# SyncE in program order, the finished inverse loaded by GpSimd, and all cross products in a step's first half, in a bidirectional RWKV-7 layer

## The chip, the core and the metric

The kernel runs on one core of one Trainium2 chip. The metric is the device time of one execution in microseconds (us). Five engines work side by side, each with an instruction stream of its own: TensorE (PE, its weight loads are PEld), VectorE (DVE), ScalarE (ACT), GpSimd (POOL) and SyncE (SP), which here does nothing but ask for transfers between the chip's memory (DRAM) and the core.

## The reference

One layer over 128 context and 2048 latent tokens, model width 1024: a normalised and modulated input goes through one projection; half of its channels feed a bidirectional RWKV-7 scan (8 heads of 64, a state of 64 by 64 per head and direction), half a short gated convolution; both are gated, concatenated and projected back onto the residual, and a final normalisation follows.

```python
def step(S, inp):                      # in _wkv, per token, both directions
    r_t, w_t, k_t, v_t, kk_t, a_t = inp
    s_kk = jnp.einsum('bdhij,bdhj->bdhi', S, kk_t)
    S = (S * w_t[..., None, :] - s_kk[..., :, None] * (kk_t * a_t)[..., None, :]
         + v_t[..., :, None] * k_t[..., None, :])
    return S, jnp.einsum('bdhij,bdhj->bdhi', S, r_t)
...
u = jnp.concatenate([ya, yb], axis=-1) @ lp['w_out']     # in _layer
return x + gate * u, s_final
```

## The kernel before

The kernel has two phases. phase1 projects all tokens and leaves in DRAM what the second needs: the scaled keys and queries of each chunk ("ops"), the values ("vt"), gates and a bonus term ("sg", "q") and the finished convolution half ("mixT"). phase2 (line 657 on), which the change is about, scans.

The scan is done in chunks of 64 tokens. A step s of the main loop covers a tile of 128 tokens in the forward direction and one in the backward, 17 steps in all; its two halves step(s, 0) and step(s, 1) are a chunk each, in both directions, for all heads. A half multiplies the state with the chunk's keys (psw, copied into ws), begins the output (psy) and the new state (pst), applies the chunk's inverse (psu, out of zb and ws, copied into sv), and then ends pst (DVE scales it into the next sv) and psy. So a half needs the state of the half before it, and zb.

zb is the inverse of a triangular matrix in each chunk, for 16 pairs of head and direction in a half; it does not depend on the state, so it is prepared two steps ahead, in this chain:

1. cross(u, i, d) for u = s + 2, four of them (C(0) to C(3) in the loop): products of the chunk's keys and queries (psB, psX). ACT copies one part into lab; for the second of each pair (i = 1), SyncE stores the diagonal 32 by 32 blocks into DRAM as "at" (line 728); DVE masks the rest into x and abr.
2. inverse(u): SyncE loads all blocks of the step as ab (line 749, two transfers), GpSimd eliminates in 15 rounds (lines 754 to 769) and stores the inverted blocks zt by four transfers of its own queue (line 774) into "zt" in DRAM.
3. merge(s + 1), a step later: SyncE loads zb (line 829), DVE transposes its blocks into a tile of the tag ws (STREAM_TRANSPOSE), TensorE fills in the block below the diagonal (psU, copied by ACT into the ws tile, then psW, copied into zb).

turn transposes keys (psT, copied into kbt; R(0) to R(3)), load_units loads kb and x for step s + 3 (L(0), L(1); lines 699 and 701), load_v loads sv (line 863).

Into these the loop mixes independent work. piece() records a quarter of a projection job: a job multiplies one tile of 128 tokens (mr, split into the halves mh by ACT and ml by DVE) with the output weights (wo..h and wo..l) in two sums of 12 matmuls, psoc (convolution half, steps 0 to 8) or psoa (scan half, from step 9 on); DVE scales each sum (o) and adds it to the residual tile z. z has two buffers and is loaded from the input x (psoc) or from "z0", where the first half of the projection left it (psoa). Eight pieces, so two jobs, go into a step. In step 9 no job is at hand and the four weight tiles are replaced (weights(), loads at line 1003 into z buffers). F() records a stage of finish(), which normalises a finished tile of the scan (psv, psr, the y operations); its result is the input of a psoa job.

What orders the work: Queue (line 640) wraps an engine. While held is set, each instruction recorded through it gets a dependency on the one recorded before, so TensorE, VectorE and ScalarE run in the program's order; their instructions all show line 648, where Queue calls the engine. SyncE and GpSimd are not held: a scheduler places their instructions by its own simulation. Each engine takes its instructions one at a time, so what waits at the head of SyncE holds up all transfers behind it. A store and a load that touch the same place in DRAM are ordered by waits on the transfer's landing.

Of the kernel before, what the change touches and what calls it, by code (L numbers as in the profile page):

```python
# [632 lines left out]
NST = 17  # L633
# [23 lines left out]
def phase2(K):  # L657
    nc, tc, A, S = K.nc, K.tc, K.A, K.S
    G = nc.gpsimd
    V, P, T = Queue(tc, nc.vector), Queue(tc, nc.scalar), Queue(tc, nc.tensor)  # L660
    D = nc.sync.dma_start
# [82 lines left out]
    def inverse(s):  # L744

        at = S["at"][s]
        ab = tl(O.r, [128, 32, 32], "ab", 2)
        for h in range(2):
            D(ab[h * 64:h * 64 + 64].rearrange("p j i -> p (j i)"), at.rearrange("b u h j i -> (b u h) (j i)"))
# [21 lines left out]
        for c in range(2):  # L771
            for b in range(2):
                x = dst[:, b * 32 + c:b * 32 + 32:2, b * 32:b * 32 + 32]
                G.dma_start(x, zt[c * 64 + b * 32:c * 64 + b * 32 + 32])

    def first(s):
        for d in range(2):
            load_units(s, d)
        for k in UNITS:
            cross(s, *k)  # L780
            yield
            turn(s, *k)
            yield
        inverse(s)
# [40 lines left out]
    def merge(s):  # L825

        zb = tl(O.r, [128, 16, 64], "zb", 2)
        zbs[s] = zb
        D(zb[:], S["zt"][s % 3].rearrange("u h r c -> (h r) u c"))
# [21 lines left out]
    svs = {}  # L851
    ys = {}
# [12 lines left out]
    def step(s, i):  # L865
# [7 lines left out]
        if not last:  # L873
            load_v(*n)
        if n == (1, 0):
            sv = svs[n]
            for h in range(2):
                for d in range(2):
                    D(sv[HR[h], h, d], A["st0"][:, d, h::2, :])
                x = sv[HR[h], h].rearrange("r d p v -> r (d p) v")  # L880
                mn = tl(O.l, [128, 8], "mn", 2)
                V.tensor_reduce(mn[HR[h]], x, mybir.AxisListType.X, ALU.add)
                V.tensor_scalar(mn[HR[h]], mn[HR[h]], -1.0 / 64, None, ALU.mult)
                V.tensor_tensor(x, x, mn[HR[h]].unsqueeze(2).broadcast_to((64, 8, 64)), ALU.add)
# [21 lines left out]
        for h in range(2):  # L906
            P.copy(sv[HR[h], h], u[HR[h]])
        yield
        if not last:
# [32 lines left out]
        if i == 1:  # L942
            zbs.pop(s)
            for d in range(2):
# [6 lines left out]
                elif s < 8:  # L951
                    D(S["ysp"][t], ys.pop(t)[:])
# [64 lines left out]
    def project(j):  # L1017
# [23 lines left out]
        if att:  # L1041
# [8 lines left out]
            D(S["y"][t0:t0 + 128, :], z[:])  # L1050
        else:
            D(S["z0"][t0:t0 + 128, :], z[:])
        yield

    def main():
        setup_rest()
        for e in (T, V, P):
# [8 lines left out]
        def take():  # L1066
# [11 lines left out]
            z = tl(O.w, [128, 1024], "z", 2)  # L1078
            D(z[:], src[t * 128:t * 128 + 128, :])
            j = Ctx()  # L1080
            j.t, j.att, j.x, j.z, j.k, j.headed = t, att, x, z, 0, False
            j.run = project(j)
            nxt.append(j)

        def piece(n=1):
            for _ in range(n):
                if B.load:
# [3 lines left out]
                if not nxt:  # L1091
                    take()
                if not now:
                    if nxt:
                        j = nxt.pop()
                        split(j)
                        now.append(j)
                    continue
                j = now[0]
                if j.k == 2 and nxt:  # L1100
# [4 lines left out]
                if j.k == 4:  # L1105
                    run(j.run)
                    now.clear()
                    if nxt:
                        m = nxt.pop()
                        split(m, m.headed)  # L1110
                        now.append(m)
# [17 lines left out]
        def F(n=1):  # L1129

            if fin:
# [11 lines left out]
        for s in range(NST):  # L1143
# [41 lines left out]
            C(2)  # L1185
            piece()
            R(2)
            L(0)
# [15 lines left out]
            piece(2)  # L1204
            m = merge(s + 1) if s + 1 < NST else iter(())
            next(m, 0), next(m, 0)
# [8 lines left out]
        while now or nxt or waiting:  # L1215
            piece()
        for p in (O.pu, O.q, O.w, O.l, O.pt, O.pg, O.r):
# [54 lines left out]
```

## Time and profile before

| what | value |
|---|---|
| median of 3 runs | 1976.24 us (1975.0 to 1979.27) |
| profiled execution, its own time | 1986.27 us |
| its span, first to last instruction | 1984.5 us |
| mean granted TensorE clock | 0.899 |
| PE, PEld, DVE busy | 1646.4, 1439.3, 1052.3 us |
| ACT, POOL busy | 641.0, 585.6 us |
| main loop | from about 1062 us on |
| steps 2 to 8 (1162 to 1493 us) | 331 us |

In the profile a row of a window names the stretch and then busy time and count by engine. A row of the waits has the engine, what it was about to do, after the arrow what ended the wait, and total us, times and the longest. A row of the timeline is start and duration in us, engine, line, operation, out<-in, shape and count; in brackets stands the idle time just before and what ended it. SPq and POOLq are transfers asked for by SyncE and GpSimd; their duration is the asking, not the transfer.

### The profile page before, as it was taken

The numbers are of one execution on the slowest core, as the hardware profiler recorded it, in microseconds if no ns is written. First come the engines' busy times: TensorE is split into PE (matmuls) and PEld (weight loads), VectorE is DVE, ScalarE is ACT, GpSimd is POOL, SyncE is SP. The second block draws the span as 40 slices with busy tenths as digits, with TensorE's granted clock in tenths as the row PEclk, the third lists the DMA queues.
The fourth block names the chain that finished last, engine by engine and source line by source line (L and its number), as shares of the span: only waits on it lengthen the run. The fifth ranks groups of instructions, "written<-read, shape, count | busy, mean of one in ns | idle before, by whom it ended". The sixth has DMA issues, their size and how long they took to land. (4 is left out here: it accounts for less than half of the span.)

```text
span 1984.5 us, 40833 instructions
## 1 busy us (share of the span) xinstructions
PE 1646.4 (83%) x16646; PEld 1439.3 (73%) x16646; DVE 1052.3 (53%) x1883; ACT 641.0 (32%) x1284; POOL 585.6 (30%) x1096
## 2 busy tenths in 40 slices
PE   5999999999999999988985966788774657877785
PEld 3998899998899998887984754566563435665564
DVE  6988876457673637764433533344332335454454
ACT  4565543244441315541102222222222312323232
POOL 0122200012120002220450544556555553345500
PEclk8999999999999999998996887888887768888787
DMA  8899986658995536789744456566564454553322
GB/s 334 235 231 245 225 241 244 234 125 182 177 198 150 195 144 153 184 188 247 222 144 138 108 150 163 145 183 179 158 177 95 113 143 136 145 142 94 114 85 85
DMA packets 390124, 339.90 MB, mean 171 GB/s; under 512 B 284136, under 2 KB 335208, under 8 KB 375856
## 3 DMA queue, kind: packets, MB, share of 16 engines
q1 hardware_dynamic: 387760, 332.82, 61.7%
q0 software_dynamic: 2176, 4.46, 1.3%
q8 instruction: 131, 2.15, 0.5%
q14 instruction: 57, 0.47, 0.1%
HBM read 215.68 MB, written 121.52 MB: 170 GB/s over the span
## 5 line engine op out<-in xcount | busy, mean ns | idle before, releaser
L769 POOL TENSOR_TENSOR zt<-zt,ztmp 128x30 f32<-128x30 f32 (+7 forms) x510 | 210.4, 412 | 40.0
L648 PE MATMUL psU<-ws,lab 32*32 32x32 f32 x1088 | 37.3, 237 | 172.9 <-DVE ws L648 172.9
L648 DVE TENSOR_TENSOR x<-psX,mx 64x512 f32<-64x512 f32 x136 | 93.6, 688 | 150.6 <-PE psB L648 127.7
L648 PEld LDWEIGHTS psU<-ws,lab 32*32 32x32 f32 x1088 | 33.2, 150 | 181.3 <-issue 172.9
L766 POOL TENSOR_TENSOR ztmp<-ab,zt 128x60 f32<-128x60 f32 (+7 forms) x255 | 137.9, 541 | 20.0
L315 POOL TENSOR_TENSOR shk<-rawl 128x384 f32<-128x384 f32 (+1 forms) x24 | 27.1, 1131 | 319.4 <-ACT rawl L311 311.1
L758 POOL COPY dgp<-ab 128x16 f32<-128x16 f32 x17 | 4.2, 245 | 382.4 <-DMA ab<-scr_at 382.3
L648 PE MATMUL psoa<-woh,ml 128*128 128x512 f32 x136 | 67.2, 494 | 49.4 <-DVE ml L648 49.4
L648 PE MATMUL psoa<-woh,mh 128*128 128x512 f32 x136 | 69.8, 513 | 20.9 <-ACT mh L648 20.9
L648 PE MATMUL psX<-x,kb 64*64 64x128 f32 x1088 | 84.2, 285 | 0.0
L648 PEld LDWEIGHTS psB<-x,kb 64*64 64x64 f32 x1088 | 62.7, 137 | 23.1 <-issue 17.5
L648 PEld LDWEIGHTS psoa<-woh,ml 128*128 128x128 f32 x136 | 32.3, 237 | 64.1 <-DVE ml L648 56.8
L648 PE MATMUL psB<-x,kb 64*64 64x128 f32 x1088 | 74.7, 277 | 3.0 <-DVE abr L648 1.7
L648 DVE TENSOR_TENSOR o<-psoa,gl 128x512 f32<-128x512 f32 x32 | 22.1, 689 | 103.1 <-PE psoa L648 101.7
L648 DVE TENSOR_TENSOR o<-psoc,gl 128x512 f32<-128x512 f32 x32 | 22.0, 687 | 97.5 <-PE psoc L648 97.5
L648 ACT ACTIVATE o<-z 128x512 f32<-128x512 f32 x34 | 21.4, 630 | 156.7 <-issue 90.5
L159 PE MATMUL mmg<-h,w 128*128 128x384 f32 (+1 forms) x192 | 63.4, 330 | 6.5 <-ACT rawc L318 3.9
L159 PE MATMUL mmv<-h,w 128*128 128x384 f32 (+1 forms) x192 | 66.6, 347 | 2.7 <-ACT q1r L313 1.5
L159 PE MATMUL mmk<-h,w 128*128 128x384 f32 (+1 forms) x184 | 61.6, 335 | 8.2 <-DMA w<-scr_wsp 8.2
L648 PE MATMUL psoc<-woh,mh 128*128 128x512 f32 x136 | 65.1, 479 | 0.0
L159 PE MATMUL mmgb<-h,w 128*128 128x384 f32 (+1 forms) x192 | 63.7, 332 | 1.5 <-DMA w<-scr_wsp 1.5
L160 PE MATMUL mmv<-h,w 128*128 128x384 f32 (+1 forms) x192 | 64.8, 337 | 0.0
(298 smaller groups left out, 5366.8 us busy)
## 6 DMA issues: line engine op xcount, KB each, us to landing
w<-scr_wsp SPq DMA_DIRECT2D x68, 1024.0 KB, 7.3
scr_wsp<-w SPq DMA_DIRECT2D x34, 1024.0 KB, 6.3
wr<-in_win SPq DMA_DIRECT2D x34, 512.0 KB, 6.9
kb<-scr_ops SPq DMA_DIRECT2D x34, 512.0 KB, 5.0
x<-scr_ops SPq DMA_DIRECT2D x68, 256.0 KB, 6.6
scr_ops<-sp SPq DMA_DIRECT2D x80, 192.0 KB, 4.6
scr_ops<-sp SPq DMA_DIRECT2D x160, 96.0 KB, 5.1
ab<-scr_at SPq DMA_DIRECT2D x34, 256.0 KB, 4.0
```

Of the source, the lines that this page charges most:

```text
L159: T.matmul(ps[:, :n], w[:, 0, k], hh[:, 0, k, :n], start=k == 0, stop=False)
L160: T.matmul(ps[:, :n], w[:, 0, k], hh[:, 1, k, :n], start=False, stop=False)
L315: G.tensor_tensor(s[:, lo:n].rearrange("p (r c) -> p r c", c=64), rp[:, :R, 0:64], rp[:, :R, 2:66], ALU.add)
L648: r = f(*args, **kw)
L758: G.tensor_copy(dg[:], ab[:].rearrange("p j i -> p (j i)")[:, 1:1024:66])
L766: G.tensor_tensor(tv, ab[:, j:j + 2, j + 2:32].unsqueeze(1).broadcast_to((128, kn, 2, n)), zt[:, :kn, j:j + 2].unsqueeze(3).broadcast_to(( ...
L769: G.tensor_tensor(zt[:, :kn, j + 2:32], zt[:, :kn, j + 2:32], tv[:, :, r], ALU.add)
```

## The change

- SyncE becomes a Queue too and is held from main() on: its transfers are asked for in the order in which the program records them.
- The program's order is rewritten for that: load_v stands behind the u to sv copies of a half, the residual z of a job is loaded by base() at the k = 1 of the job before it (or in ready()), fetch(u), the ab load, is split off inverse(u) and recorded after the psu of the second half and a piece, stores of z0, y and ysp are collected in late and recorded by flush() at the next piece; L(0) and L(1) move back a little; the mean that is subtracted from the first state is computed after the first psu.
- inverse(u) ends with the load of zb on GpSimd's own queue, behind the four stores of zt; merge only picks the tile up.
- C(3) and R(3) go ahead of step(s, 1).
- merge's transposes are recorded ahead of two pieces instead of behind them, one more F() follows psU, head() of the next job comes at k = 3 instead of 2, and ready() lets F() begin a job.

```diff
@@ phase2
-    V, P, T = Queue(tc, nc.vector), Queue(tc, nc.scalar), Queue(tc, nc.tensor)
-    D = nc.sync.dma_start
+    V, P, T, SP = Queue(tc, nc.vector), Queue(tc, nc.scalar), Queue(tc, nc.tensor), Queue(tc, nc.sync)
+    D = SP.dma_start
...
-    def inverse(s):
-
-        at = S["at"][s]
+    def fetch(s):
         ab = tl(O.r, [128, 32, 32], "ab", 2)
         for h in range(2):
-            D(ab[h * 64:h * 64 + 64].rearrange("p j i -> p (j i)"), at.rearrange("b u h j i -> (b u h) (j i)"))
+            D(ab[h * 64:h * 64 + 64].rearrange("p j i -> p (j i)"), S["at"][s].rearrange("b u h j i -> (b u h) (j i)"))
+        return ab
+
+    def inverse(s, ab):
+
         zt = tl(O.r, [128, 16, 32], "zt", 1)
...
                 G.dma_start(x, zt[c * 64 + b * 32:c * 64 + b * 32 + 32])
+        zb = tl(O.r, [128, 16, 64], "zb", 2)
+        zbs[s] = zb
+        G.dma_start(zb[:], S["zt"][s % 3].rearrange("u h r c -> (h r) u c"))
...
     def merge(s):
 
-        zb = tl(O.r, [128, 16, 64], "zb", 2)
-        zbs[s] = zb
-        D(zb[:], S["zt"][s % 3].rearrange("u h r c -> (h r) u c"))
+        zb = zbs[s]
...
+    late = []
+
+    def flush():
+        while late:
+            late.pop(0)()
@@ step
-        if not last:
-            load_v(*n)
-        if n == (1, 0):
...
         for h in range(2):
             P.copy(sv[HR[h], h], u[HR[h]])
+        if not last:
+            load_v(*n)
...
-                    D(S["ysp"][t], ys.pop(t)[:])
+                    late.append(lambda t=t, y=ys.pop(t): D(S["ysp"][t], y[:]))
@@ project
-            D(S["y"][t0:t0 + 128, :], z[:])
-        else:
-            D(S["z0"][t0:t0 + 128, :], z[:])
+        late.append(lambda: D(S["y" if att else "z0"][t0:t0 + 128, :], z[:]))
@@ main
-        for e in (T, V, P):
+        for e in (T, V, P, SP):
             e.held = True
...
+        def base(j):
+
+            j.z = tl(O.w, [128, 1024], "z", 2)
+            D(j.z[:], j.src[j.t * 128:j.t * 128 + 128, :])
+
+        def ready():
+            if not nxt:
+                take()
+            if not now and nxt:
+                j = nxt.pop()
+                if j.z is None:
+                    base(j)
+                split(j, j.headed)
+                now.append(j)
+
         def piece(n=1):
             for _ in range(n):
+                flush()
...
-                if j.k == 2 and nxt:
+                if j.k == 1 and nxt:
+                    base(nxt[0])
+                if j.k == 3 and nxt:
                     nxt[0].headed = True
                     head(nxt[0])
...
         def F(n=1):
 
+            if not B.load:
+                ready()
@@ main, the loop over s
             C(2)
+            R(2)
             piece()
-            R(2)
-            L(0)
+            C(3)
+            R(3)
             F()
             a = step(s, 1)
             next(a), next(a)
-            C(3)
-            if u:
-                inverse(u)
-            R(3)
-            L(1)
+            L(0)
             F()
             next(a)
             piece()
+            if u:
+                ab = fetch(u)
+                inverse(u, ab)
+            L(1)
             F()
             piece()
             next(a), next(a)
             F()
+            m = merge(s + 1) if s + 1 < NST else iter(())
+            next(m, 0)
             piece(2)
-            m = merge(s + 1) if s + 1 < NST else iter(())
-            next(m, 0), next(m, 0)
+            next(m, 0)
+            F()
             piece(2)
             next(m, 0)
             piece()
```

The order on SyncE in step 4, which prepares u = 6. The names have running numbers; at is the store of blocks, lab its source. Before, from just behind the first at store on:

```order
L699 DMA kb_1423_12777<-scr_ops0_57 128x2x512
L1052 DMA scr_z0_68<-z_1396_12387 128x1024
L701 DMA x2_1424_12778<-scr_ops0_57 64x2x512 x2
L701 DMA x3_1434_12921<-scr_ops1_59 64x2x512 x2
L1071 DMA mr_1435_12944<-scr_mixT_64 128x4x128
L1079 DMA z_1436_12946<-in_x 128x1024
L829 DMA zb_1442_13024<-scr_zt_66 128x16x64
L728 DMA scr_at_65<-lab_1414_12680 32x8x32 x4
L699 DMA kb_1433_12920<-scr_ops1_59 128x2x512
L863 DMA sv_1449_13129<-scr_vt_61 64x2x256
L952 DMA scr_ysp_67<-y_1417_12727 128x512
L749 DMA ab_1428_12851<-scr_at_65 64x1024 x2
```

And now, from that first at store on:

```order
L648 DMA scr_at_65<-lab_1414_12642 32x8x32 x4
L648 DMA scr_z0_68<-z_1392_12330 128x1024
L648 DMA scr_at_65<-lab_1418_12695 32x8x32 x4
L648 DMA kb_1429_12862<-scr_ops0_57 128x2x512
L648 DMA x2_1430_12863<-scr_ops0_57 64x2x512 x2
L648 DMA sv_1431_12886<-scr_vt_61 64x2x256 x2
L648 DMA z_1432_12889<-in_x 128x1024
L648 DMA ab_1434_12900<-scr_at_65 64x1024 x2
L648 DMA kb_1439_12964<-scr_ops1_59 128x2x512
L648 DMA x3_1440_12965<-scr_ops1_59 64x2x512 x2
L648 DMA scr_ysp_67<-y_1421_12742 128x512
```

The two at stores have moved together, with a z0 store between them, and ab follows behind one kb, one x, sv and one z load; zb is gone from SyncE, where the second at store and ab stood behind it.

The order on VectorE at the end of step 4, around the transposes of the next step's zb (STREAM_TRANSPOSE, made for psU of step 5). Before:

```order
L648 TENSOR_TENSOR o_1438_12962<-psoc80_12949,gl_10178 128x512
L648 TENSOR_TENSOR z_1405_12507<-z_1405_12507,o_1438_12962 128x512
L648 TENSOR_TENSOR sv_1425_12782<-pst41_12821,pc_10168 64x512 x2
L648 TENSOR_TENSOR o_1440_13018<-psoc81_13005,gl_10178 128x512
L648 TENSOR_TENSOR z_1405_12507<-z_1405_12507,o_1440_13018 128x512
L648 TENSOR_TENSOR ml_1441_13022<-mr_1435_12944,mh_1439_13003 128x512
L648 STREAM_TRANSPOSE ws_1443_13026<-zb_1442_13024 32x512 x2
L648 TENSOR_TENSOR o_1447_13082<-psoc90_13069,gl_10178 128x512
L648 TENSOR_TENSOR z_1436_12946<-z_1436_12946,o_1447_13082 128x512
```

And now:

```order
L648 TENSOR_TENSOR o_1433_12897<-psoc80_12782,gl_10182 128x512
L648 TENSOR_TENSOR z_1407_12517<-z_1407_12517,o_1433_12897 128x512
L648 TENSOR_TENSOR sv_1431_12886<-pst41_12859,pc_10172 64x512 x2
L648 STREAM_TRANSPOSE ws_1441_13012<-zb_1398_12403 32x512 x2
L648 TENSOR_TENSOR o_1443_13025<-psoc81_12969,gl_10182 128x512
L648 TENSOR_TENSOR z_1407_12517<-z_1407_12517,o_1443_13025 128x512
L648 TENSOR_TENSOR ml_1444_13028<-mr_1413_12622,mh_1442_13017 128x512
L648 TENSOR_TENSOR o_1448_13084<-psoc90_13034,gl_10182 128x512
L648 TENSOR_TENSOR z_1432_12889<-z_1432_12889,o_1448_13084 128x512
```

The transposes have moved ahead of the end of the job of tile 8 (psoc81) and of the split of the next job's input (ml); before, they stood behind both. The same sv operation stands ahead of them.

The order on VectorE in step 12, from the masks of the last cross products to the next job's input; the z operation with fg is the final scaling of a psoa job. Before:

```order
L648 SCALAR_TENSOR_TENSOR y_1690_16467<-y_1690_16467,gwh_10162,psr11_17313 128x128 x4
L648 TENSOR_TENSOR y_1690_16467<-y_1690_16467,sg_1742_17134 128x512
L648 TENSOR_TENSOR y_1690_16467<-y_1690_16467,mr_1743_17135 128x512
L648 TENSOR_TENSOR x5_1721_16848<-psX1411_17373,mx_8877 64x4x2x64 x2
L648 TENSOR_TENSOR abr11_1762_17395<-psB1411_17372,mx_8877 128x256
L648 RECIPROCAL rs_1770_17478<-rs_1770_17478 128x8
L648 TENSOR_TENSOR o_1772_17508<-psoa71_17294,gl_10178 128x512
L648 TENSOR_TENSOR z_1729_16957<-z_1729_16957,o_1772_17508 128x512
L648 TENSOR_TENSOR ss_1736_17035<-ss_1736_17035 128x1
L648 RECIPROCAL ss_1736_17035<-ss_1736_17035 128x1
L648 SCALAR_TENSOR_TENSOR z_1729_16957<-z_1729_16957,ss_1736_17035,fg_1676_16268 128x1024
L648 TENSOR_TENSOR ml_1774_17519<-y_1690_16467,mh_1773_17517 128x512
```

And now:

```order
L648 TENSOR_TENSOR o_1756_17316<-psoa71_17090,gl_10182 128x512
L648 TENSOR_TENSOR z_1735_16997<-z_1735_16997,o_1756_17316 128x512
L648 TENSOR_TENSOR ss_1737_17037<-ss_1737_17037 128x1
L648 RECIPROCAL ss_1737_17037<-ss_1737_17037 128x1
L648 SCALAR_TENSOR_TENSOR z_1735_16997<-z_1735_16997,ss_1737_17037,fg_1660_16076 128x1024
L648 TENSOR_TENSOR x5_1729_16908<-psX1411_17325,mx_8877 64x4x2x64 x2
L648 TENSOR_TENSOR abr11_1757_17347<-psB1411_17324,mx_8877 128x256
L648 SCALAR_TENSOR_TENSOR y_1691_16476<-y_1691_16476,gwh_10166,psr11_17358 128x128 x4
L648 TENSOR_TENSOR y_1691_16476<-y_1691_16476,sg_1742_17140 128x512
L648 TENSOR_TENSOR y_1691_16476<-y_1691_16476,mr_1743_17141 128x512
L648 TENSOR_TENSOR ml_1767_17423<-y_1691_16476,mh_1766_17421 128x512
```

The end of the job of tile 7 (psoa71, z with fg) has moved ahead of the x5 mask and of the y operations of finish; ml of the next job stands at the end as before.

More of the change, by code (lines that the diff above doesn't have):

```diff
@@ L783, in first @@
             yield
-        inverse(s)
+        inverse(s, fetch(s))
     def early():
@@ L1108, in piece @@
                     if nxt:
[L1109 to L1111 removed]
+                        ready()
         def head(j):
```

33 lines of the change are left out of this document (15 added, 18 removed).

## The prediction

> **What bounds the kernel now.** First the page: one execution, its span 1984.5 us.
>
> ```profile
> span 1984.5 us, 40833 instructions
> ```
>
> Then the windows, cut where a step of the main loop begins (steps 0–1, 2–8, 9, 10, 11–14, 15 with the tail). The columns are the stretch, its us, busy PE, PEld, DVE, ACT, POOL with counts, the granted clock, the DMA share and GB/s.
>
> ```profile
> 1070.00:1162.00 92.00, 76.50 (x1318) 60.88 (x1319) 41.53 (x70) 25.86 (x50) 26.75 (x56) 0.84 0.48 122
> 1162.00:1493.00 331.00, 247.09 (x4514) 198.91 (x4508) 123.85 (x193) 84.36 (x167) 184.30 (x394) 0.86 0.60 162
> 1493.00:1562.00 69.00, 29.79 (x612) 23.92 (x612) 18.18 (x27) 14.33 (x23) 42.11 (x84) 0.66 0.41 104
> 1562.00:1633.00 71.00, 43.95 (x674) 33.96 (x672) 29.37 (x52) 16.86 (x37) 40.02 (x81) 0.78 0.49 123
> 1633.00:1865.00 232.00, 179.01 (x2689) 140.15 (x2688) 113.63 (x208) 67.40 (x144) 111.08 (x222) 0.82 0.47 127
> 1865.00:1984.50 119.50, 85.39 (x977) 67.46 (x976) 57.77 (x113) 33.56 (x75) 1.85 (x3) 0.84 0.28 89
> ```
>
> No engine is full: in steps 2–8, 331/7 = 47.3 us each, TensorE is idle 84 us, and POOL, which computes the inverses, idles 147. The waits of that stretch (us in total, times, longest) name the partners:
>
> ```profile
> POOL dgp L758 <- DMA ab<-scr_at: 115.6, 8, 24.9
> PE psU L648 <- DVE ws L648: 75.4, 14, 18.8
> SPq L829 <- DMA scr_zt<-zt: 62.0, 7, 17.0
> ```
>
> 75.4 of TensorE's 84 idle us lie before one place, psU, which waits for DVE's transposes of zb, the finished inverse. And POOL waits for its next input, ab, while SyncE stands on the zb load. One turn of the timeline shows that these close a loop:
>
> ```profile
> 1347.27 2.98 SPq L728 DMA_DIRECT2D scr_at<-lab  x4
> ...
> 1392.11 0.38 SPq L829 DMA_DIRECT2D zb<-scr_zt  x1
> 1392.71 2.56 SPq L749 DMA_DIRECT2D ab<-scr_at  x2
> ```
>
> ```profile
> 1358.90 0.20 POOL L758 COPY dgp<-ab 128x16 f32<-128x16 f32 x1 [11.20 <-DMA ab<-scr_at]
> ...
> 1385.95 2.65 POOL L774 DMA_DIRECT2D scr_zt<-zt  x4 [0.30 <-POOL zt L769]
> 1392.09 0.53 POOL L754 MEMSET zt<- 128x512 f32 x1 [3.49 <-DMA scr_zt<-zt]
> 1400.09 0.20 POOL L758 COPY dgp<-ab 128x16 f32<-128x16 f32 x1 [7.13 <-DMA ab<-scr_at]
> ```
>
> The ab of the next inverse is asked for only at 1392.71, right behind the zb of this one. So a turn is ab's trip, POOL's 27.05 us (1358.90 to 1385.95), the stores' landing, and then the same again: 1400.09 − 1358.90 = 41 us here, in which POOL works for 27. POOL is a partner in the loop, not a full engine.
>
> **The step without the loop.** The same turn on TensorE:
>
> ```profile
> 1362.23 1.15 PE L648 MATMUL psw<-sv,x 128*64 128x64 f32 x32
> ...
> 1372.73 0.50 PE L648 MATMUL psoc<-woh,mh 128*128 128x512 f32 x1
> ...
> 1374.22 0.60 PE L648 MATMUL psT<-idt,kb 128*128 128x128 f32 x4
> ...
> 1398.73 0.28 PE L648 MATMUL psU<-ws,lab 32*32 32x32 f32 x2 [10.26 <-DVE ws L648]
> ...
> 1401.21 0.80 PE L648 MATMUL psoc<-woh,mh 128*128 128x512 f32 x1
> ...
> 1406.63 1.21 PE L648 MATMUL psW<-zb,ws 32*32 32x32 f32 x64
> ...
> 1409.36 1.15 PE L648 MATMUL psw<-sv,x 128*64 128x64 f32 x32
> ```
>
> The step is 47.13 us (1362.23 to 1409.36), 10.26 of it the wait. Behind the wait twelve psoc matmuls take 5.42 us (0.45 each); six undisturbed ones took 1.49 (0.25). So the cold clock costs 12 × 0.20 = 2.4, and the warm work is 47.13 − 10.26 − 2.4 = 34.4 us.
>
> What the wait has hidden comes out. DVE has this chain between the last matmul of one projection job and the first of the next:
>
> ```profile
> 1384.72 1.38 DVE L648 TENSOR_TENSOR sv<-pst,pc 64x512 f32<-64x512 f32 x2
> 1388.51 0.69 DVE L648 TENSOR_TENSOR o<-psoc,gl 128x512 f32<-128x512 f32 x1 [2.41 <-PE psoc L648]
> 1389.24 0.69 DVE L648 TENSOR_TENSOR z<-z,o 128x512 f32<-128x512 f32 x1
> 1389.85 0.68 DVE L648 TENSOR_TENSOR ml<-mr,mh 128x512 fp32r<-128x512 f32 x1
> ```
>
> 0.69 + 0.69 + 0.68 = 2.06, now bare once a step, since matmuls of the next job stand ahead of psU and want ml; and I keep 2.0 of the 2.4 for a half clock that such a gap may still cause. T0 = 34.4 + 2.06 + 2.0 = 38.5 us a step.
>
> **The change, part by part.** SyncE in program order with the ab load behind both at stores, the cross products in the first half, and zb on GpSimd together set a new trip, counted from a step's first psw. C(3) ends where the order puts it: C(2) ended 10.5 in (1372.73), then psT 0.6, a piece 1.5, C(3) about 1.1, the lab copy 0.6: the stores are issued at 14.3. Store issue to POOL's start 11.63 (1347.27 to 1358.90, a turn where nothing stood between); POOL 27.05; its stores until POOL goes on 6.14 (1385.95 to 1392.09); the issue of zb on GpSimd and its landing:
>
> ```profile
> L774 POOL DMA_DIRECT2D scr_zt<-zt x68: 648/648/812, 989.2 to 1866.2; - x68
> ```
>
> ```profile
> zb<-scr_zt SPq DMA_DIRECT2D x17, 512.0 KB, 4.7
> ```
>
> No GpSimd load of zb is in the trace; I take one store's 0.65 us and SyncE's landing of 4.7. The bounds: its issue could be as much as all four stores, 2.65, and its other terms 1.7 shorter where the stores land sooner. Sum 14.3 + 11.63 + 27.05 + 6.14 + 0.65 + 4.7 = 64.5 (62.8 to 66.5). The transposes stand 23.9 into the next step (behind the sv pair, done at 1386.10 in a step begun at 1362.23). A wait W lengthens both the step in which the trip runs and that in which it ends: 2W = 64.5 − 38.5 − 23.9 = 2.1, W = 1.0, T = 39.5 (37 to 42, the lower end with no half clock and no wait, the upper with 66.5 and a second bare gap). POOL itself needs 27.05 + 6.14 + 0.65 = 34 a turn, and 39 if it stands for zb's landing too: near T, not above. Steps 2–8 gain 7 × (47.3 − 39.5) = 55; steps 0–1, without the full loop, 92 − 81 = 11; the weights' loads that merge(0) waits for, 3.
>
> The Trainium skill, SBUF — State Buffer, section "A bandwidth-pool intuition that's wrong (but worth ruling out)", speaks against zb on GpSimd: a DMA of GpSimd of some 620 ns alone takes some 3100 beside a copy on VectorE, as its descriptors must wait. The 68 stores above, made while DVE ran tensor_tensors, are 648 to 812 ns, so the trace does not show it; by the rule the sum would be (3.1 − 0.65)/2 = 1.2 more a step, an estimate from that page, 9 us in all.
>
> Steps 9 and 10 have their own rows, first waits, then SyncE's issues:
>
> ```profile
> PE psU L648 <- DVE ws L648: 39.2, 4, 35.7
> ...
> PE psoa L648 <- DVE ml L648: 19.3, 2, 14.8
> ```
>
> ```profile
> 1524.32 0.37 SPq L829 DMA_DIRECT2D zb<-scr_zt  x1
> ...
> 1540.69 1.01 SPq L1003 DMA_DIRECT2D z<-in_wout  x2
> ...
> 1596.78 0.54 SPq L1044 DMA_DIRECT2D fg<-in_fg  x1
> ```
>
> In step 9 the transposes stand on DVE behind the halves of the new weights, whose last two loads were issued only at 1540.69, behind zb, at, kb, x and ab. With zb off SyncE they go when their buffers are free, and the 35.7 us go; what is late next is POOL's trip or the weights' own chain of loads and copies, so I take 47 rather than 40: 69 − 47 = 22. In step 10 the final scaling waited for fg, issued behind ab; in program order it stands between the step's two at stores, ahead of x, sv and ab (the first of the order's places has the same at stores), about 10 us sooner than 1596.78, an estimate by SyncE's place in a step: 14.8 goes nearly whole, with its cold clock: 71 − 54 = 17.
>
> Steps 11–14 wait elsewhere:
>
> ```profile
> PE psoa L648 <- DVE ml L648: 23.2, 8, 5.0
> PE psoa L648 <- ACT mh L648: 13.2, 4, 3.3
> ```
>
> 36.4 us in four steps of 58 at a clock of 0.82. At one of the two job boundaries of a step the job's end on DVE now stands ahead of the last cross products, and TensorE has those to do meanwhile; the other stays, and z now comes by a later load. I take half of the two rows and of the cold clock behind them, 7 a step: 58 to 51 (bounds 46 and 57), 4 × 7 = 28. Step 15 and the tail, where no inverse is left: 2.5. Deferred stores, the state-mean and the extra F() I take at nothing: SyncE stands on a z store's landing ahead of a z load already now, and the at stores come later; without that cover it is one landing, about zb's 4.7, on the trip, 2.4 a step.
>
> Sum: 3 + 11 + 55 + 22 + 17 + 28 + 2.5 = 138.5. The profiled execution took 1986.27; less 138.5 it is 1847.8. The median of the runs, 1976.24, is 0.995 of it: 1838 us.
>
> **The rivals.** (a) The loop stays the bound on POOL's side: GpSimd's zb load holds POOL until landing and the next ab comes in its shadow, T = 43. For it: POOL's 34–39. Against: the ab of the next step is asked for 50 us ahead. Steps 2–8 then gain 30 instead of 55, step 9 about 16: 1838 + 25 + 6 = 1869. (b) The attention steps gain nothing: VectorE's chain and the z load asked at k = 1 stay last at both boundaries: 1838 + 28 = 1866. (c) No half clock is left and the late steps reach 46: 7 × 2.5 + 4 × 5 = 37 less, 1801. The Trainium skill, TensorE: Matmul & The Clock Gate, section "HAM oscillation — how this bites in real kernels", would let the clock drop only behind gaps above some 3.4 us, which favours (c); the trace has not decided it for gaps of 2 us. (d) Slower: SyncE in program order is a single file. The z0 store, which waits for DVE, stands ahead of at stores, and mr ahead of sv; if such a data wait delays at and ab by D, the trip grows by D and a step by D/2. It decides against the change when D passes 2 × 7.8 = 16 us in steps 2–8; at 25 us they lose 7 × 4.7 = 33, steps 9–14 gain half of 67 at most, and with sv or kb late too, nothing: 2009. For it: SyncE stood 62 us on a data wait before. Against: in the new order the z0 store between the at stores belongs to a job whose last DVE operations stand ahead of the step's first cross product. (e) TensorE's wait is not for zb's loop but returns elsewhere, as ml and mh waits, and nothing shows: 1976.
>
> **How the numbers follow.** Forecast 0.58, (a) 0.12, (b) 0.12, (c) 0.08, (d) 0.06, (e) 0.04. The forecast's own bounds (T 37 to 42, late steps 46 to 57) give 1806 to 1868. Low 1800 takes in (c); high 1880 takes in (a) and (b); (d) and (e) are out. A measurement of this kernel tells 0.2%, 4 us, from no change: faster 0.90, same 0.04, slower 0.06.
>
> **What would show it.** Right: psU's wait in steps 2–8 falls from 75.4 to under 20 us, POOL's wait for ab to under 60, the zb load's issue on GpSimd is under 1 us, steps are 39.5 us, and no 35.7 or 14.8 us wait is left in steps 9 and 10. A zb issue near 3 us, or steps of 43 with POOL always busy, is (a); ml and mh waits above 30 us in steps 11–14 is (b). The prediction is wrong if SyncE's longest waits are for DVE's z while POOL stands on ab, or if psU still waits 8 us a step.

## The result, and the profile after

The changed kernel takes 1920.65 us in the median of 4 runs (1913.59 to 1922.74), the kernel before 1977.76 in runs on the same chips (1975.0 to 1987.64): ratio 0.9696, 95% interval 0.9654 to 0.9739. It is faster by 57 us; the forecast was faster by 138, to 1838, with a range of 1800 to 1880. The direction came, and 41% of the size.

The profiled execution took 1919.48 us, its span is 1917.7. The windows of after, cut at the same steps as those of before (0 to 1, 2 to 8, 9, 10, 11 to 14, 15 with the tail):

```profile
1065.00:1159.00 94.00, 79.34 (x1318) 62.35 (x1320) 42.10 (x71) 26.36 (x51) 35.63 (x74) 0.84 0.63 153
1159.00:1471.00 312.00, 236.20 (x4512) 187.60 (x4506) 124.61 (x193) 82.82 (x167) 197.12 (x405) 0.87 0.61 161
1471.00:1525.00 54.00, 31.82 (x618) 25.35 (x618) 19.97 (x29) 15.20 (x26) 32.19 (x66) 0.76 0.59 147
1525.00:1580.00 55.00, 40.98 (x676) 32.44 (x678) 28.22 (x52) 16.92 (x37) 25.71 (x53) 0.84 0.60 154
1580.00:1794.00 214.00, 162.78 (x2688) 128.18 (x2688) 114.82 (x208) 67.46 (x144) 118.41 (x235) 0.84 0.54 139
1794.00:1917.70 123.70, 87.31 (x970) 68.31 (x970) 57.03 (x111) 32.97 (x74) 12.62 (x24) 0.82 0.30 92
```

Set against the rows of before, with what the forecast gave each term:

| stretch | before, us | after, us | gain | forecast |
|---|---|---|---|---|
| up to step 0 | 1070 | 1065 | 5 | 3 |
| steps 0 and 1 | 92 | 94 | −2 | 11 |
| steps 2 to 8 | 331 | 312 | 19 | 55 |
| step 9 | 69 | 54 | 15 | 22 |
| step 10 | 71 | 55 | 16 | 17 |
| steps 11 to 14 | 232 | 214 | 18 | 28 |
| step 15 and tail | 119.5 | 123.7 | −4 | 2.5 |
| sum | 1984.5 | 1917.7 | 67 | 138.5 |

The two spans differ by 67 us, the medians by 57: the profiled execution of before was 10 us above its median. Of the 72 us that are missing in the profile 36 lie in steps 2 to 8. There six of the seven steps now come in pairs, 52 to 54 us and then 35 to 36; the last takes 47.7, the mean is 44.6. One step of 36 us and the one of 53 behind it from the timeline, first SyncE in the step that begins at 1210.7:

```profile
1224.76 2.61 SPq L648 DMA_DIRECT2D scr_at<-lab  x4
1227.47 0.40 SPq L648 DMA_DIRECT2D kb<-scr_ops  x1
1228.03 1.23 SPq L648 DMA_DIRECT2D x<-scr_ops  x2
1229.64 1.71 SPq L648 DMA_DIRECT2D sv<-scr_vt  x2
1231.39 0.59 SPq L648 DMA_DIRECT2D z<-in_x  x1
1232.10 1.11 SPq L648 DMA_DIRECT2D ab<-scr_at  x2
```

The inverse of that ab on GpSimd, begun near the end of this step, and then, in the next one (begun at 1246.8), the transposes it releases on VectorE and what TensorE waits for:

```profile
1242.64 0.66 POOL L760 COPY dgp<-ab 128x16 f32<-128x16 f32 x1 [18.96 <-DMA ab<-scr_at]
...
1270.05 2.62 POOL L776 DMA_DIRECT2D scr_zt<-zt  x4 [0.30 <-POOL zt L771]
1279.20 1.16 POOL L779 DMA_DIRECT2D zb<-scr_zt  x1 [6.54 <-DMA scr_zt<-zt]
...
1281.30 0.20 POOL L760 COPY dgp<-ab 128x16 f32<-128x16 f32 x1
```

```profile
1285.07 1.42 DVE L648 STREAM_TRANSPOSE ws<-zb 32x512 f32<-32x512 f32 x2 [14.13 <-DMA zb<-scr_zt]
1286.51 0.69 DVE L648 TENSOR_TENSOR o<-psoc,gl 128x512 f32<-128x512 f32 x1
1287.24 0.82 DVE L648 TENSOR_TENSOR z<-z,o 128x512 f32<-128x512 f32 x1
1287.98 0.83 DVE L648 TENSOR_TENSOR ml<-mr,mh 128x512 fp32r<-128x512 f32 x1
```

```profile
1288.87 0.79 PE L648 MATMUL psoc<-woh,ml 128*128 128x512 f32 x1 [16.23 <-DVE ml L648]
```

Over steps 2 to 8 the waits are these:

```profile
PE psoc L648 <- DVE ml L648: 54.4, 6, 17.2
PE psU L648 <- DVE ws L648: 14.2, 2, 13.8
POOL dgp L760 <- DMA ab<-scr_at: 49.6, 3, 19.0
```

What the reader is to see: most of the wait has changed its name, from psU for the transposes (75.4 us before) to psoc for ml, because the transposes now stand ahead of the job's end on VectorE and hold it. Its cause is the same zb, and with 68.6 us in both rows it has hardly shrunk. What steps 2 to 8 gained is 8 us of TensorE's idle time (84 to 76 in the windows) and 11 us of its busy time (247 to 236). And the trip of the inverse, from the step's first psw to the transposes, is 1285.07 − 1210.7 = 74.4 us where the prediction had 64.5. GpSimd went on to the next inverse 2.1 us after it asked for zb; its wait for ab, 18.96 here, is one of the long kind of before. The median landings of the loads in the whole run, KB and us, before first:

```profile
kb<-scr_ops SPq DMA_DIRECT2D x34, 512.0 KB, 5.0
x<-scr_ops SPq DMA_DIRECT2D x68, 256.0 KB, 6.6
...
ab<-scr_at SPq DMA_DIRECT2D x34, 256.0 KB, 4.0
```

and after:

```profile
kb<-scr_ops SPq DMA_DIRECT2D x34, 512.0 KB, 8.2
x<-scr_ops SPq DMA_DIRECT2D x68, 256.0 KB, 8.6
...
ab<-scr_at SPq DMA_DIRECT2D x34, 256.0 KB, 8.2
zb<-scr_zt POOLq DMA_DIRECT2D x17, 512.0 KB, 6.1
```

Program order asks for kb, x, sv, z and ab, 2.25 MB, within 6 us, and kb, x and ab land later than before. That gives theory A: the change is limited by its own burst of loads, which makes the trip 10 us longer. Its rivals: B, GpSimd's part of the trip is what is long (the landing of its stores, the asking for zb); C, SyncE in single file costs by its waits or by the place that a transfer has in it.

### The profile page after: what moved, and what is told of

The parts are those of the page before. It is cut to its first block, busy times and chain, and to the rows that moved or that the text cites. A ratio compares the mean times of both kernels' runs of the same rounds, so it can differ in the third digit from the quotient of the medians.

```text
span 1917.7 us, 40711 instructions
## 1 busy us (share of the span) xinstructions
PE 1622.0 (85%) x16646; PEld 1416.9 (74%) x16646; DVE 1057.2 (55%) x1883; ACT 640.4 (33%) x1284; POOL 604.5 (32%) x1113
## 5 line engine op out<-in xcount | busy, mean ns | idle before, releaser
L648 PE MATMUL psoc<-woh,ml 128*128 128x512 f32 x136 | 59.2, 435 | 67.8 <-DVE ml L648 67.0
L648 PE MATMUL psU<-ws,lab 32*32 32x32 f32 x1088 | 32.1, 226 | 84.4 <-DVE ws L648 84.4
L648 PEld LDWEIGHTS psU<-ws,lab 32*32 32x32 f32 x1088 | 29.0, 141 | 92.7 <-issue 88.2
L648 PEld LDWEIGHTS psoc<-woh,ml 128*128 128x128 f32 x136 | 28.5, 209 | 78.1 <-DVE ml L648 70.5
L648 PE MATMUL psoa<-woh,ml 128*128 128x512 f32 x136 | 64.2, 472 | 22.5 <-DVE ml L648 22.5
L648 DVE TENSOR_TENSOR z<-z,o 128x512 f32<-128x512 f32 x68 | 51.6, 758 | 32.3 <-DMA z<-scr_z 23.1
L159 PE MATMUL mmv<-h,w 128*128 128x384 f32 (+1 forms) x192 | 65.7, 342 | 1.1 <-ACT q1r L313 0.6
```

The lines of the kernel that those rows point to most:

```text
L159: T.matmul(ps[:, :n], w[:, 0, k], hh[:, 0, k, :n], start=k == 0, stop=False)
L648: r = f(*args, **kw)
```

## The experiments

Each kernel is the changed one with the edit shown; "..." stands for lines left out. Times are medians beside the kernel before on the same chip, whose medians were 1982.5 to 1984.4 us in these sessions; so compare the ratios.

**Ab asked for first** (e1) and **kb and x last** (e2):

```diff
             C(3)
             R(3)
+            ab = fetch(u) if u else None
...
             if u:
-                ab = fetch(u)
                 inverse(u, ab)
```

```diff
             next(a), next(a)
-            L(0)
...
                 inverse(u, ab)
+            L(0)
             L(1)
```

> The changed kernel with one move: the ab load is recorded right behind the last cross product's turn, ahead of kb, x, sv and z. Theory A (the trip of an inverse is 74 us instead of 64.5 because ab is asked for last in a burst of loads, and lands in 8 to 10 us instead of 4 to 6): ab is asked for about 3 us sooner and lands in under 6, the trip is about 66, steps 2 to 8 fall from 44.6 to about 40 us, the whole by 25 to 35 us to 1887 to 1896. Theory B (the trip is long because of GpSimd's own part: the landing of its stores, then the issue of zb): at most the 3 us of the earlier asking come off the trip, half of that off a step, 1908 to 1920.

> The changed kernel with the first kb and x loads moved behind the ab load, to the second ones; sv and z stay ahead of ab. Theory A (a burst of loads delays what stands at its end): ab lands in 5 to 7 us, half of the gain of asking for ab first, and in steps 11 to 14 the z load, now ahead of kb and x, lands in time, so that the waits for DVE before psU there (30.6 us in four steps) fall under 12: in all 20 to 40 us, 1881 to 1901. Theory B (GpSimd's own part): nothing beyond 5 us in steps 2 to 8; late steps as under A.

e1: 1907.08 us, 0.9601 (0.9578 to 0.9623), some 19 us better than the change. Ab landed in 3.7 us in the median, and GpSimd started 26.6 us into a step instead of 33.2, as A says; but zb, now asked for beside the next step's ab, kb and x, landed in 7.2 instead of 6.1, and steps 2 to 8 came to 42.8 us, not 40, so that the time lies between what A and B had said. e2: 1890.78 us, 0.9515 (0.9482 to 0.9547), 36 us better; steps 11 to 14 fell from 53.5 to 49.5, with 16.8 us before psU, not under 12. Steps 2 to 8 hardly moved (44.3), although GpSimd started 28.0 us into a step and zb landed 3.5 us sooner: TensorE was busy for 247.5 us in them instead of 236.5, and why is left open. What stands behind the burst is late, ab or zb or, in the late steps, z.

**Zb on SyncE again**, at merge's place (e3) and ahead of the burst (e9):

```diff
     def inverse(s, ab):
...
-        G.dma_start(zb[:], S["zt"][s % 3].rearrange("u h r c -> (h r) u c"))
...
     def merge(s):
...
+        D(zb[:], S["zt"][s % 3].rearrange("u h r c -> (h r) u c"))
```

```diff
             C(3)
             R(3)
             F()
             a = step(s, 1)
             next(a), next(a)
+            if s + 1 < NST:
+                bring(s + 1)
             L(0)
```

In e9, bring(s) holds the D(zb) line that e3 has in merge.

> The changed kernel with the zb load back on SyncE at the place of merge; SyncE still in program order, ab still behind both at stores. Theory A: the trip keeps its burst; zb itself lands in 4.7 instead of 6.1 and GpSimd saves an issue of 1.16 us, so steps 2 to 8 are 43 to 45 us and the whole 1905 to 1925. Theory B (GpSimd's part is what costs): steps near 41 us, 1890 to 1900. Theory C (SyncE in single file, held by the wait for zb, holds mr and at behind it): steps of 47 us and more, 1940 or above.

> As the run with zb back on SyncE, but the zb load stands behind the second at store, ahead of kb, x, sv, z and ab, instead of behind them all. If it was the place in the single file that cost the 82 us (zb asked for some 20 us after its inverse was stored), most of it comes back: steps 2 to 8 of 43 to 47 us, 1915 to 1955. If any zb load on SyncE closes the old loop again (ab of the next inverse behind zb of this one), steps are 47 us or more: 1975 or above.

e3: 2001.94 us, 1.0075 (1.005 to 1.01): all of the change but zb's engine is slower than before, by under 1%. Steps 2 to 8 are 50.3 us. It is C, but not by a wait; it is the place. GpSimd and SyncE of e3 in the step that begins at 1229.9:

```profile
1240.90 0.53 POOL L756 MEMSET zt<- 128x512 f32 x1 [1.83 <-DMA scr_zt<-zt]
```

```profile
1250.30 1.11 SPq L648 DMA_DIRECT2D ab<-scr_at  x2
1251.44 0.59 SPq L648 DMA_DIRECT2D kb<-scr_ops  x1
1252.55 1.87 SPq L648 DMA_DIRECT2D x<-scr_ops  x2
1254.60 0.46 SPq L648 DMA_DIRECT2D zb<-scr_zt  x1
```

The inverse lies in memory at 1240.9, and SyncE comes to its load 13.7 us later, behind both at stores, the burst and a second kb and x, without standing for zb. e9: 1962.6 us, 0.9892 (0.9862 to 0.9923), between its two cases, with steps of 47.5. With zb ahead, ab is behind it, and the old loop is closed again, in the step begun at 1259.3:

```profile
1275.77 1.84 SPq L648 DMA_DIRECT2D scr_at<-lab  x4
1289.70 0.38 SPq L648 DMA_DIRECT2D zb<-scr_zt  x1
...
1294.67 1.11 SPq L648 DMA_DIRECT2D ab<-scr_at  x2
```

SyncE stood 12 us on zb with kb, x, sv, z and ab behind it. In one file, either zb is behind the burst or ab is behind zb.

**SyncE not held** (e4): the scheduler places its transfers, zb stays on GpSimd.

```diff
-        for e in (T, V, P, SP):
+        for e in (T, V, P):
```

> The changed kernel, but SyncE not held: the scheduler places its transfers again; zb stays on GpSimd and all else in the order of the change. If zb off SyncE is what brought the gain, it stays at 1910 to 1930; if program order on SyncE brought it, the time goes back above 1950. By theory A the loads are spread again and ab lands in under 6 us, so that it could even be faster than the changed kernel where ab is not asked for later.

1896.83 us, 0.9532 (0.9498 to 0.9567), faster than the change by some 32 us. With e3 and e9 that says: the gain needs zb on GpSimd, and program order on SyncE, as written here, costs. Zb on GpSimd alone, in the kernel before, was not run, so what it is worth without the rest of the change is not shown.

**The fourth cross product back** behind the start of the second half (e5), and **every x load twice** (e7, the same bytes to the same place):

```diff
-            C(3)
-            R(3)
             F()
             a = step(s, 1)
             next(a), next(a)
+            C(3)
+            R(3)
             L(0)
```

```diff
-        for h in range(2):
+        for h in (0, 1, 0, 1):
             D(x[HR[h], :, h].rearrange("r i a p t -> r i (a p t)"), src[HR[h], :, 0:512])
```

> The changed kernel with the fourth cross product and its turn put back behind the start of the second half. If the trip of the inverse sets steps 2 to 8, its at stores and with them all that follows come 4 to 5 us later in a step, a step gets about half of that longer, 2 to 2.5 us, in 9 steps about 20 us: 1935 to 1945. If the burst of loads is what ab waits for anyway, the later cross product is hidden: 1915 to 1925.

> The changed kernel with every x load issued twice (the same bytes into the same place; 0.5 MB more before each ab load, and 1.2 us more of asking). Theory A: ab is asked for 1.2 us later and lands 2 to 3 us later, POOL starts 3 to 4 us later, steps 2 to 8 grow by 1.5 to 2.5 us, late steps by 1 to 3 as their z load lands later too: 1940 to 1955. If the landing of ab does not hang on the loads ahead of it: only the asking, 1920 to 1930.

e5: 1936.01 us, 0.9754 (0.972 to 0.9787), the trip 2.2 us longer, steps 46.7: the early cross products are worth some 11 us. e7: 1978.97 us, 0.9979 (0.9959 to 1.0): the whole gain is gone, twice what A said. But the edit adds more than bytes. The second pair of x loads writes the place of the first, and SyncE, in single file, stands until the first has landed. First one row of four x loads, which spans such a wait, then SyncE's waits for x in steps 2 to 8, 6.1 us in the changed kernel:

```profile
1251.17 8.91 SPq L648 DMA_DIRECT2D x<-scr_ops  x4
```

```profile
SPq L648 <- DMA x<-scr_ops: 96.0, 26, 9.8
```

So ab was asked for 27.8 us into a step instead of 21.2, and from there to GpSimd's start it took 10.2 us, no longer than the 12.0 of the changed kernel. e7 does not show how a longer burst lands; it shows what a longer trip costs, 81.1 us against steps of 47.7.

**The burst taken apart** (e6): ab first as in e1, the first kb and x at the end of the second half, the second behind psU.

```diff
             a = step(s, 1)
             next(a), next(a)
-            L(0)
...
                 inverse(u, ab)
-            L(1)
             F()
             piece()
             next(a), next(a)
             F()
+            L(0)
             m = merge(s + 1) if s + 1 < NST else iter(())
...
             next(m, 0)
             F()
+            L(1)
             piece(2)
```

> Ab asked for right behind the last cross product, as in the run with ab first, and the loads of kb and x taken apart: the first pair at the end of the second half, the second behind psU. Theory A (bursts of loads delay whatever stands behind or beside them, ab at first, and zb once ab is ahead): ab lands in about 4 us and zb in about 6 instead of 7 to 12, the trip is 64 to 66 us, steps 2 to 8 are 40 to 41.5 us, in steps 11 to 14 the z load lands in time, 49 us: 1870 to 1885. If kb and x now come too late for the next step's cross products, waits of psB for a load show up instead, and the time is above 1895. Theory B (GpSimd's own part is what is long): steps 2 to 8 stay at 42 to 43 us.

1866.88 us, 0.9428 (0.9391 to 0.9466), 53 us better than the change. Steps 2 to 8 are 40.8 us at a clock of 0.90, and GpSimd's wait for ab has shrunk from 115.6 us before and 49.6 in the changed kernel to 38.7. The windows of these steps and of steps 11 to 14:

```profile
1156.00:1442.00 286.00, 240.35 (x4514) 190.94 (x4512) 125.74 (x193) 83.93 (x167) 194.33 (x399) 0.90 0.66 174
...
1537.00:1738.00 201.00, 159.17 (x2692) 125.42 (x2694) 115.27 (x208) 67.55 (x144) 118.81 (x233) 0.89 0.55 148
```

Zb stayed on GpSimd with all its costs, and the trip fell from 74.4 to 66.0 us; B is left with what remains over 64.5.

**The late steps.** In steps 11 to 14 another load is behind the burst, the residual z. SyncE and VectorE of the changed kernel in step 12:

```profile
1657.72 0.58 SPq L648 DMA_DIRECT2D z<-scr_z  x1
```

```profile
1660.72 0.69 DVE L648 TENSOR_TENSOR o<-psoa,gl 128x512 f32<-128x512 f32 x1 [3.54 <-PE psoa L648]
1668.50 0.69 DVE L648 TENSOR_TENSOR z<-z,o 128x512 f32<-128x512 f32 x1 [7.09 <-DMA z<-scr_z]
...
1673.66 1.43 DVE L648 STREAM_TRANSPOSE ws<-zb 32x512 f32<-32x512 f32 x2
```

z, asked for 3 us before VectorE wants it, lands 10.8 us later, and sv, the y operations and the transposes queue up behind; TensorE then waits 8.30 us before psU. Three repairs on e6 together (e10), the second of them alone on the changed kernel (e11), and the load moved (e13 on the changed kernel, e14 on e10):

```diff
@@ e10 (1): step, for the first state (moved here from behind the u to sv copies)
+        if n == (1, 0):
+            load_v(*n)
+            x0 = svs[n]
+            for h in range(2):
+                for d in range(2):
+                    D(x0[HR[h], h, d], A["st0"][:, d, h::2, :])
         sv = svs.pop((s, i))
@@ e10 (2) and e11: the transposes ahead, from step 10 on
             next(a)
+            m = None
+            if 9 < s < NST - 1:
+                m = merge(s + 1)
+                next(m, 0)
             piece()
@@ e10 (3): behind the loop, with no ready() in F there
         while fin:
             F()
-            piece()
+            if not now and (nxt or waiting):
+                ready()
+            else:
+                piece()
@@ e13 and e14: z of a step's first new job, at the step's start; base() takes it from pre
+            if s > 10 and fin and not nxt:
+                flush()
+                t = fin[0][0]
+                pre[t] = tl(O.w, [128, 1024], "z", 2)
+                D(pre[t][:], S["z0"][t * 128:t * 128 + 128, :])
             a = step(s, 0)
```

> The spread loads and three more repairs, each in a stretch of its own. (1) The load of the first state stands at the start of step 0's second half again, ahead of the burst: the 10.7 us that psoc waits for ml in step 0 go, 8 us. (2) From step 10 on the transposes of zb stand on DVE ahead of the job's end, which waits for the z load: the 4.6 us wait before psU goes and some of the cold clock behind it, steps 11 to 14 fall from 50 to about 46 us, 20 to 25 us with step 10. (3) Behind the loop a job's split counts as a piece of its own again, as before the change, so that a stage of finish comes between: the 7 us that the tail has lost come back. In all 1867 less 35 to 40: 1827 to 1832. If the late wait only moves from the transposes to ml (the next thing behind z on DVE), (2) brings 5 us and the whole is near 1847.

> The changed kernel with (2) alone: from step 10 on the transposes of zb ahead of the job's end on DVE. If the late z load is felt because the transposes stand behind it, the waits before psU (30.6 us in steps 11 to 14) go and these steps fall from 53.5 to 47 or 48: 1890 to 1897. If ml, further behind on DVE, then holds psoa instead: 1905 to 1918.

> The changed kernel with one load moved: from step 11 on the residual z of a step's first new job is loaded at the step's start, ahead of sg, mr and the burst, instead of behind kb and x. If this load, landing some 10 us after it is asked for, is what sv, the y operations, the transposes and ml wait for on DVE in the late steps, then the waits there (30.6 us before psU and 10.5 for ml in steps 11 to 14) fall under 15, steps 11 to 14 go from 53.5 to 46 or 47, and the whole is 1885 to 1895. If DVE's own chain of finish and job end is what bounds these steps, they stay at 51 us or more, 1910 or above.

> The run with all repairs and this z load at the step's start as well. If the z load bounds the late steps there too (49.3 us), they fall to 44 to 46, 15 to 20 us in steps 11 to 14: 1840 to 1846. If DVE's chain binds: 1855 to 1862.

e11: 1924.58 us, 0.9699 (0.9673 to 0.9724): nothing, above both of its cases. The wait moved, to ml as the second case said and more so to mh on ScalarE; steps 11 to 14, after and then e11:

```profile
PE psU L648 <- DVE ws L648: 30.6, 8, 8.4
PE psoa L648 <- DVE ml L648: 10.5, 4, 2.8
```

```profile
PE psoa L648 <- ACT mh L648: 25.0, 4, 8.6
PE psoa L648 <- DVE ml L648: 15.7, 4, 4.1
```

e13: 1902.03 us, 0.9586 (0.9561 to 0.9611), some 22 us better than the change by moving one load, 7 short of its expectation; steps 11 to 14 come to 48.7 us, with 46 in two of them and 53 and 49 in the others, where the transposes now wait for zb (4.6 us in the two). This row of VectorE's waits in steps 11 to 14 of the changed kernel is gone in e13 and e14:

```profile
DVE z L648 <- DMA z<-scr_z: 15.4, 3, 7.1
```

e10: 1860.04 us, 0.9388 (0.9362 to 0.9415), 8 us better than e6, with intervals that overlap, and not 35 to 40. (1) did nothing: step 0 is 49.7 us, since the first state is asked for 23.4 us into it, 22.5 in the changed kernel, and VectorE still does its mean ahead of the transposes. (2) moved the wait. (3) brought some 5 us from step 15 on. e14: 1853.45 us, 0.9333 (0.9311 to 0.9356), the fastest here: steps 11 to 14 are 45.9 us. Both show the z load to be what held these steps, for some 20 us in the changed kernel and 12 in e10; the whole of e14 is 7 us above its expectation.

**All repairs with SyncE not held** (e12, as e4 on e10):

> All repairs, but SyncE not held, so that the scheduler places its transfers. If a written order on SyncE is worth having once ab is first and the loads are spread, this is slower than the held one by 10 us or more (ab behind loads again); if the order hardly matters as long as zb is off SyncE, both are within 6 us.

1884.16 us, 0.9491 (0.9473 to 0.9509), slower than e10 by 1%, some 20 us. A written order on SyncE is worth having once it is the right one.

## Why the prediction was wrong, by its own steps

**The mechanism and its formula held, one term of it was mis-sized.** The prediction had the wait of a step from trip, work and the place of the transposes: 2W = trip − T0 − 23.9. Only the sum of two steps' waits is fixed by that; a long step makes the next one short, which is why they can pair (in e7, with the longest trip, they are all near 47.7). In the short ones (35.0 us, clock 1.00) nothing waits for zb:

```profile
1300.00:1335.00 35.00, 32.93 (x654) 26.20 (x652) 18.13 (x29) 11.54 (x24) 15.10 (x29) 1.00 0.74 188
```

With T0 = 35.5 instead of 38.5, the transposes at 23.6, and 1.2 us a step for the cold clock behind each second wait (half of 2.4), T = 35.5 + (trip − 59.1)/2 + 1.2. These constants were read from the changed kernel, so its own row is no test, but the other rows are. The trips, from the starts of the steps to zb's landing, mean over steps 2 to 8 (the forecast's ab is 14.3 and the 5.46 from the at stores to ab in its turn):

| kernel | ab asked | POOL starts | stores of zt | zb asked | zb landed | T by the formula | T measured |
|---|---|---|---|---|---|---|---|
| forecast | 20 | 25.9 | 53.0 | 59.1 | 64.5 | 39.4 | |
| changed | 21.2 | 33.2 | 60.3 | 67.9 | 74.4 | 44.4 | 44.6 |
| e1, ab first | 20.1 | 26.6 | 53.8 | 60.7 | 69.7 | 42.0 | 42.8 |
| e2, kb and x last | 21.1 | 28.0 | 55.2 | 61.8 | 70.9 | 42.6 | 44.3 |
| e5, cross back | 23.7 | 34.1 | 61.2 | 68.9 | 76.6 | 45.5 | 46.7 |
| e7, x twice | 27.8 | 38.0 | 64.7 | 72.5 | 81.1 | 47.7 | 47.7 |
| e6, spread | 20.0 | 25.5 | 52.7 | 58.2 | 66.0 | 40.2 | 40.8 |

With the forecast's own 38.5 and 23.9 these trips give 44.5 (changed), 42.2 (e1), 42.8 (e2), 45.6 (e5), 47.9 (e7) and 40.3 (e6), so it is the trip that was missing, and not the constants. e2 lies 1.5 us or more off either way, e5 about 1.2, the others under 1.

So the step that failed is the trip's term "store issue to POOL's start 11.63". The at stores went out as forecast (14.0 to 16.1 us into a step), and ab was asked for nearly when the forecast had it; but from there to GpSimd's start it took 12.0 us instead of 6.2. The 11.63 came from a turn of before "where nothing stood between". That reading was wrong too: SyncE's rows of that turn have kb, a sv and two ysp stores between the at stores and ab (1350.35 to 1352.73), only no x and no z. The new order showed kb, x, sv and z there, and the forecast gave their landing no time. POOL's start came 7.3 us later than forecast, the stores' landing until zb is asked for added 1.4, zb's landing 1.2. e6, where no load stands between, has the forecast's 25.9 within half a us, and its 40.8 us a step lie in the forecast's 37 to 42. e1, e2 and e6 are what shows theory A; in all of them GpSimd starts 5 to 8 us sooner than in the changed kernel.

- **T0** was 3 us too high: in the three short steps the chain o, z, ml leaves a gap of 1.83 to 1.85 us, and the half clock that I kept for it did not come there. The error did little harm: it makes T 1.5 us too long, and the cold clock behind the second waits, 1.2 us a step, was left out.
- **The signs** were mixed. POOL's wait for ab is 49.6 us, under 60, and psU's 14.2, under 20, but the wait went to psoc; zb's request took 1.16 us, not under 1. SyncE's longest waits are for DVE's z, which was to be a sign of failure:

```profile
SPq L648 <- DVE z L648: 57.0, 4, 16.2
```

These waits end 40 to 43 us into a step, behind the at stores and ab, so they are not what held GpSimd.

- **zb on GpSimd** was right as the gain: without it the rest of the change is slower than before (e3) or 1% faster (e9). Its asking measured 1162 ns, between the forecast's 0.65 and its bound of 2.65. The Trainium skill, SBUF — State Buffer, section "A bandwidth-pool intuition that's wrong (but worth ruling out)", gives some 3100 for a request beside a copy on VectorE. The 17 requests measured 1162 to 1174; VectorE was at work beside 13 of them (and beside 35 of the 68 stores that the forecast went by), nearly always with tensor_tensors, so the page's own case is hardly tested here. Rival (a), GpSimd held until the landing, did not come: the next inverse began 2.1 us after the request.
- **Rival (d)**, SyncE's single file, was right in kind and wrong in its place. Not the waits for VectorE delayed at and ab; what cost was the room that loads without a deadline took ahead of those with one. The Trainium skill, DMA: Bandwidth & Descriptors, section "Issuing engines are not separate DMA queues", says that transfers share the same 16 engines whoever asks, and that a second issuing engine saves only the time of asking. The landings agree with the first half (e1: ab sooner, zb later). The second half does not hold here: the other issuing engine was worth some 75 us against e3 (ratios 1.0075 and 0.9696) and 39 against e9 (0.9892), because it changed what stood ahead of zb and of ab.
- **Steps 9 and 10**: the 35.7 and 14.8 us went, as forecast; 31 of 39 us came.
- **Steps 11 to 14**: 18 of 28 us. Rival (b) named it, "the z load asked at k = 1"; e13 and e14 show that it is that load and that moving what waits behind it (e11) is nothing.
- **Steps 0 and 1**: the mean of the first state, which I took at nothing, now stands ahead of the transposes on VectorE and waits for its own load; psoc waits 10.7 us there for ml. (1) of e10 left it asked for as late, so how much of these steps it costs stays open.
- **The tail** lost 7 us behind step 16's start. In the three kernels with (3) this stretch is 78.5 (e10), 73.4 (e12) and 75.6 us (e14), in all others of the changed kind 79 to 83, before 74.5: that the split of a job now comes ahead of a stage of finish is most of it, as far as single profiles tell.

Why e14 is 7 us above what I expected was not followed up.

## What to carry to other kernels

When transfers of one engine are put into program order, cost the landing of the load that matters behind everything asked for just ahead of it, not by a turn with fewer loads in it; then ask for the load with the tightest deadline first and spread those that have half a step to spare. Here a load that waited for GpSimd's results did best on GpSimd, since what stood behind it in SyncE's file fed the same loop. Where two stages wait for each other across iterations, only the sum of neighbouring waits is fixed: take the mean of a pair before judging a step, and use the short one to read the true work.

## What the runs showed of the hardware that was not expected

- A request on GpSimd for the load of zb (128 x 16 x 64, 512 KB) took 1162 to 1174 ns, one for a store of 64 KB 649; from the start of the request zb landed in 5.8 us at the least from GpSimd (changed) and 4.4 from SyncE (before, where the request took 0.37), in spite of the same size.
- The same 256 KB load of ab landed in 8.2 us in the median behind kb, x, sv and z, and in 3.7 ahead of them (e1).
- Behind gaps of nearly the same length TensorE's clock went both ways: after 1.85 us it stayed at 1.00 (the window above) and the psU behind took 1.20 us; after 1.83 us in step 1, where it had been at 1.00 for 20 us, the psU behind took 1.91:

```profile
1326.91 0.50 PE L648 MATMUL psoc<-woh,ml 128*128 128x512 f32 x1 [1.85 <-DVE ml L648]
...
1328.03 1.20 PE L648 MATMUL psU<-ws,lab 32*32 32x32 f32 x64
...
1147.86 0.50 PE L648 MATMUL psoc<-woh,ml 128*128 128x512 f32 x1 [1.83 <-DVE ml L648]
...
1148.99 1.91 PE L648 MATMUL psU<-ws,lab 32*32 32x32 f32 x64
```
